# Second layer of an mLSTM / sparse-attention trunk: low parts, scale products, compression products and a mask spread on other places

## The chip, the cores and the metric

One core of one Trainium2 chip. The time is device microseconds of one execution; it is the median of the runs that is compared. The profile is of one execution, and its times are microseconds from the start of the span, unless marked ns.

## The reference

Two layers over 256 tokens of 1024 channels, all float32; then a last norm. Each layer adds a mixer of the normed input:

```python
for i in range(DEPTH):            # DEPTH = 2
    if i % 2 == 0: x = x + mlstm_mixer(rmsnorm(x, ml_norm), ...)
    else:          x = x + nsa_mixer(rmsnorm(x, nsa_norm), ...)
return rmsnorm(x, final_norm)
```

The mLSTM mixer projects to 2 x 2048 channels, convolves, makes q, k and v of four heads, mixes them with exponential gates and projects back with a weight of 2048 x 1024 (the first output projection). The second mixer projects to queries (16 heads of 64), three pairs of keys and values (4 groups of 64), a gate path z and gate logits. One pair is compressed, blocks of 32 tokens at a step of 16:

```python
def compress(t, pe, w1, w2):
    blocks = t[:, tok_idx] + pe[:, None, :]
    flat = blocks.transpose(0, 1, 3, 2, 4).reshape(B, n_cmp, G, CMP_BLOCK * DK)
    return jax.nn.silu(flat @ w1) @ w2
k_cmp = compress(k_c, cmp_pe[0], cmp_w1[0], cmp_w2[0])
v_cmp = compress(v_c, cmp_pe[1], cmp_w1[1], cmp_w2[1])
```

Attention over the compressed pair, over selected blocks and over a window is gated per head, summed, multiplied by SiLU of z and projected by 1024 x 1024.

## The kernel before, in words

Weights come in 44 units of 1 MB or less, each in two halves, through rings of raw tiles (four halves) and of converted tiles (five). `load_unit` issues the load of a half on SyncE's queue (L282); ScalarE rounds it to fp32r, the high part (L283); the low part, raw minus high, is made in one of two ways. Either VectorE subtracts (L289), or ScalarE writes the negated copy (L286) and GpSimd issues a DMA that adds the raw tile to it (L287). The list `BY_DMA` names the halves of the second way. A product of two float32 matrices is then three fp32r products: high by high, low by high, high by low. `next_unit` has two units loaded ahead of the one in use.

Units 0 to 15 are the input projection of the first layer, 16 to 23 its output projection (`out_project`, products at L745, evacuation with the residual at L769). The second layer takes units in the order of `ORDER`: 24 and 25 are the compressed keys and values (`project_tokens`, L828 to L831), 26 to 31 keys and queries in pairs (`heads8`, through `project_channels`, L429), 32 to 35 values and gates, 36 to 39 z, 40 to 43 the output projection.

The norm's factor of a token isn't applied to h: h is x transposed (L345) times the norm's gain, in a high (L350) and a low part (L351), and the factor multiplies the results. `token_scale` makes it by a power on GpSimd (L334), and `token_rows` makes it a row on all partitions by a product of ones with diagonals (L387, L388); rb, rb8, rbh and rp are copies of it, whole, by 1/8, by 1/2 and by the parity of the token.

In `heads8` the first 16 channels of each head are turned: a copy (L852), four small DMAs into a swap tile (L856, on SyncE's queue), two products (L857, and L858 on GpSimd) and an add (L859). There is one swap tile.

`compressed_keys_values` evacuates units 24 and 25 (L1017), transposes, adds the positions into a tile of flat blocks (L1036), multiplies by the first compression weight (L1039) for the keys and then for the values, into the two halves of the partitions of one bank, and so on to a tile `vbd`, in which each group's values are spread over its four heads by a mask (L1066). A plain product of float32 is run in two passes, so one of them stands as two instructions.

The order of instructions on each engine is made by the framework's planner from the program's order and its own estimate of times; `behind(a, b)` sets a after b on their engine, without a semaphore.

Of the kernel before, what the change touches and what calls it, by code (L numbers as in the profile page):

```python
# [12 lines left out]
OP = mybir.AluOpType  # L13
# [3 lines left out]
P = 128  # L17
# [20 lines left out]
MORE = 4  # L38
CG = 1
GV = ((0, 0, 0),)  # L40
VB = 0
NSW = 1

LAG = (0, 4)
# [2 lines left out]
TR = ((0, 0),)  # L47

YH = ((3, 1),)
RBA = 3  # L50
TV = (('px', 'px'), ('acc0', 'acc1'))
TC = ('px', 'px')
TK = (('acc0', 'px'),) * 3
# [10 lines left out]
EDGES = ((1, 8), (1, 32))  # L64
XTH = 2
NOT_POOL = (0, 1, 2, 11)
BOTH = (15, 16, 17)
BY_DMA = [(i, 1) for i in list(range(24)) + list(range(24, 48, 2)) if i not in NOT_POOL] + [(i, 0) for i in BOTH]


WI1 = range(16)
# [136 lines left out]
def trunk(ctx, tc, a, out, dbg=None):  # L208
# [14 lines left out]
    def T(*x, **k):  # L223
        return tile_of(pool[0], *x, **k)
# [42 lines left out]
    def load_unit(src, row, nk, nn):  # L267

        hk = nk // 2
        halves = []  # L270
        for i in range(2):
            raw = TS([P, hk, nn], tag="wr", bufs=WR)
            hi = TS([P, hk, nn], F32R, tag="wh", bufs=WH)
            lo = TS([P, hk, nn], F32R, tag="wl", bufs=WH)
            parts = 1 if loaded else 2
            for j in range(parts):
                if not loaded:
                    load_x(2 * i + j)
                w = hk // parts
                k = slice(j * w, (j + 1) * w)  # L280
                o = i * hk + j * w
                nc.sync.dma_start(raw[:, k, :].rearrange("p k n -> p (k n)"), src[row * P:(row + 1) * P, o * nn:(o + w) * nn])  # L282
                A.activation(hi[:, k, :], raw[:, k, :], AF.Copy)  # L283
                if (len(loaded), i) in BY_DMA:

                    A.activation(lo[:, k, :], raw[:, k, :], AF.Copy, scale=-1.0)  # L286
                    GP.dma_start(out=lo[:, k, :].rearrange("p k n -> p (k n)"), in_=raw[:, k, :].rearrange("p k n -> p (k n)"), accum_op=OP.add)  # L287
                else:
                    V.tensor_tensor(lo[:, k, :], raw[:, k, :], f32(hi[:, k, :]), op=OP.subtract)  # L289
            halves.append((hi, lo))  # L290
        return halves
# [33 lines left out]
    GP.memset(mhalf, -0.5)  # L325


    def rstd_of(ms, n, name):

        k = ms.shape[1]  # L330
        me = T([P, k], name=name + "me")
        V.tensor_scalar(me, ms, 1.0 / n, 1e-6, op0=OP.mult, op1=OP.add)
        r = T([P, k], name=name)
        GP.tensor_tensor(r, me, mhalf[:, 0:k], op=OP.pow)  # L334
        return r

    ahead(N0)
# [9 lines left out]

    def scaled(kts, at, gain):
        for kt in kts:
            A.activation(hh[:, kt, :], at(kt), AF.Copy, scale=gain[:, kt:kt + 1])  # L350
            V.scalar_tensor_tensor(hl[:, kt, :], at(kt), gain[:, kt:kt + 1], f32(hh[:, kt, :]),  # L351
                                   op0=OP.mult, op1=OP.subtract)

# [25 lines left out]

    last = [None]  # L380

    def token_rows(r, bank, **place):

        dg = T([P, 2, P], name="dg", **place)
        ps = PS((P, S), tag=bank)
        for tb in range(2):
            V.tensor_scalar(dg[:, tb, :], ident, r[:, tb:tb + 1], None, op0=OP.mult)  # L387
            last[0] = PE.matmul(ps[:, tb * P:(tb + 1) * P], onesq, dg[:, tb, :], start=True, stop=True)  # L388
        return ps, dg

    held = {}
    rb1 = T([P, S], name="rb1")
    rb1h = T([P, S], name="rb1h")

# [400 lines left out]
    pool[0] = ctx.enter_context(tc.tile_pool(name="s2", bufs=1))  # L795
    transposed(range(4, 8), x_cols, gain2)
    r2 = token_scale(ss2, "r2")
    ps, dg = token_rows(r2, "acc0", tag="p0", bufs=PB)
    rb = T([P, S], name="rb")
    V.tensor_copy(rb, ps)  # L800
    rb8 = T([P, S], name="rb8")
    if RBA & 1:
        A.activation(rb8, ps, AF.Copy, scale=0.125)
    else:
        V.tensor_scalar(rb8, ps, 0.125, None, op0=OP.mult)
    rbh = T([P, S], name="rbh")
    if RBA & 2:
        A.activation(rbh, ps, AF.Copy, scale=0.5)
    else:
        V.tensor_scalar(rbh, ps, 0.5, None, op0=OP.mult)  # L810
    rp = T([P, 2], name="rp")
    V.tensor_tensor(dg, rb.rearrange("p (s r) -> p r s", r=2), ident[:, None, :].to_broadcast([P, 2, P]), op=OP.mult)
    V.tensor_reduce(rp, dg, axis=AX.X, op=OP.add)

    def project_tokens(units, nn, tokens, evac, tags=("px", "px")):

        ps = [PS(tag=t) for t in tags]
        for i, (src, r_) in enumerate(units):
            halves = next_unit(src, r_, nn)
            for k0, low in ((0, False), (0, True), (2, False), (2, True)):  # L820
                for k in (k0, k0 + 1):
                    kt = 4 * i + k
                    hi, lo = halves[k // 2]
                    for t in range(2):
                        lh, ll = tokens(hh, kt, t), tokens(hl, kt, t)
                        o_ = ps[t][:, 0:nn]
                        if low:
                            PE.matmul(o_, lh, lo[:, k % 2, :], start=False, stop=kt == KT - 1)  # L828
                        else:
                            PE.matmul(o_, lh, hi[:, k % 2, :], start=kt == 0, stop=False)  # L830
                            PE.matmul(o_, ll, hi[:, k % 2, :], start=False, stop=False)  # L831
        for t in range(2):
            evac(t, ps[t][:, 0:nn])

# [5 lines left out]
    nc.scalar.dma_start(trig.rearrange("p a s -> p (a s)"), a["rope"])  # L840
    swaps = [T([P, 2, S], name="swap") for _ in range(NSW)]
    for t in swaps:
        GP.memset(t, 0.0)
    turn = lambda i: trig[:, i, None, :].to_broadcast([P, 2, S])

    def heads8(row, rbt, out, n, tags=("px", "px")):
# [167 lines left out]
    def compressed_keys_values():  # L1014
        cs = T([P, 2, G, 2, 64], tag="khl", bufs=2, name="cs")
        project_tokens([(a["wi2"], 0), (a["wi2"], 1)], 512, parity,
                       lambda t, ps: A.activation(cs[:, :, :, t, :], ps.rearrange("p (v g d) -> p v g d", v=2, g=G), AF.Copy,  # L1017
                                                  scale=rp[:, t:t + 1]), tags=TC)
        w1t = []
        for kv in range(2):  # L1020
            for hf in range(2):
# [2 lines left out]
                w1t.append(t)  # L1024
        pe_ = CB("pe").rearrange("p (v l) -> p v l", v=2)
        hps = PS((P, P), tag="acc1")
        for kv in range(2):
            ps = PS((P, G, P), tag="pt")
            for g in range(G):
                PE.transpose(ps[:, g, :], cs[:, kv, g, :, :].rearrange("p r d -> p (r d)"), ident)  # L1030
            f = T([P, 16, G, 16], tag="cf", name="fl")
            GP.memset(f, 0.0)
            for g in range(G):
                src = ps[:, g, 0:128].rearrange("p (c l) -> p l c", l=8)
                for lh_ in range(2):
                    V.tensor_tensor(f[:, 8 * lh_:8 * lh_ + 8, g, 0:15], src[:, :, lh_:lh_ + 15],  # L1036
                                    pe_[:, kv, 8 * lh_:8 * lh_ + 8, None].to_broadcast([P, 8, 15]), op=OP.add)
            for lp in range(16):
                PE.matmul(hps[64 * kv:64 * kv + 64, :], f[:, lp, :, :].rearrange("p g c -> p (g c)"),  # L1039
                          w1t[2 * kv + lp // 8][:, lp % 8, :], start=lp == 0, stop=lp == 15)  # L1040
        h1 = T([P, P], tag="t1", bufs=3, name="h1")
        V.tensor_copy(h1, hps)
# [6 lines left out]
        ps = PS((P, P), tag="acc1")  # L1049
        PE.transpose(ps, h1, ident)  # L1050
        V.tensor_copy(h1T, ps)
        GP.memset(kcb, 0.0)
        ps = PS((P, G, 16), tag="acc1")
        PE.matmul(ps.rearrange("p g c -> p (g c)"), CB("w2k"), h1T[:, 0:64], start=True, stop=True)
        for r in range(2):
# [7 lines left out]
        vc = [T([P, G, 64], F32R, name="vc") for _ in range(2)]  # L1063
        split(*vc, ps)
        for b_, v_ in zip(vbd, vc):
            (GP, V)[VB].tensor_tensor(b_, f32(v_)[:, :, None, :].to_broadcast([P, G, 4, 64]),  # L1066
                             C("hmask")[:, None, :, None].to_broadcast([P, G, 4, 64]), op=OP.mult)

# [128 lines left out]
```

## Time and profile before

| | |
|---|---|
| median of 3 runs | 373.99 us (372.49 to 377.45) |
| the profiled execution | 371.21 us |
| its span | 369.4 us |
| mean granted clock of TensorE | 0.982 of full speed |

The span goes from the first instruction to the last; the time of the execution has what lies around it. A matmul's end is modelled, so the shown idle time before the next one is a lower bound of the time lost.

### The profile page before, as it was taken

How to read it: one execution, taken by the hardware profiler on the slowest of the kernel's cores; microseconds unless marked ns; L12 is line 12 of the kernel's file. 1: busy time of each engine (PE TensorE's matmuls, PEld its weight loads, DVE VectorE, ACT ScalarE, POOL GpSimd, SP SyncE). 2: the span in 40 equal slices, each digit the busy share in tenths (PEclk: the TensorE clock that was granted, in tenths of full speed). 3: DMA queues.
4: the chain of work that ended last, by engine and by line, in shares of the span. 5: the costliest groups of instructions: out<-in, count | busy, mean ns of one | idle time of the engine just before them, and what ended most of it. 6: DMA issues, size and time to landing. Idle time of an engine off the chain costs nothing.

```text
span 369.4 us, 6638 instructions
## 1 busy us (share of the span) xinstructions
PE 348.2 (94%) x2399; PEld 311.4 (84%) x2399; DVE 247.4 (67%) x539; ACT 241.4 (65%) x441; POOL 108.6 (29%) x151
## 2 busy tenths in 40 slices
PE   5999999999999999997997999999699999999991
PEld 5999999999998899875886799999689986777770
DVE  3969977494786789623217547597977989594414
ACT  6755997786696769455736452644589689995304
POOL 1022131322211335010102003671720455665003
PEclk9799999999999999999999999999989999999998
DMA  7899789774569796999998977626496863030003
GB/s 228 323 338 293 221 242 316 171 213 101 188 165 194 219 220 112 267 264 255 261 254 288 301 266 192 158 78 155 134 284 195 268 199 107 2 59 0 2 0 114
DMA packets 23713, 70.62 MB, mean 191 GB/s; under 512 B 2560, under 2 KB 4992, under 8 KB 23680
## 3 DMA queue, kind: packets, MB, share of 16 engines
q1 hardware_dynamic: 17552, 49.76, 39.2%
q0 software_dynamic: 4752, 16.83, 24.9%
q10 hardware_dynamic: 1376, 3.61, 2.9%
q8 instruction: 19, 0.31, 0.3%
q14 instruction: 14, 0.11, 0.1%
HBM read 51.92 MB, written 1.05 MB: 143 GB/s over the span
## 4 chain that ended last, share of the span: by engine, by line
PE 50%; DMA 24%; ACT 11%; DVE 6%; issue 5%; SPq 1%; ACTq 0%; POOLq 0%; POOL 0%; DVEq 0%
PE ps L429 22%; DMA wl<-wr 10%; DMA wr<-in_wo_dram 6%; PE ps L745 6%; ACT wh L283 4%; DMA wr<-in_wi_dram 3%; DVE wl L289 3%; PE ps L664 2%; ACT wl L286 2%; PE ps L1039 2%; PE ps L964 2%; PE ps L952 2%; DMA wr<-in_wi2k_dram 2%; PE ps L548 2%; DMA xch<-in_xt_dram 1%
## 5 line engine op out<-in xcount | busy, mean ns | idle before, releaser
L429 PE MATMUL ps<-hT,wh 128*128 128x256 f32 x832 | 137.5, 291 | 3.4 <-ACT wh L283 3.4
L283 ACT ACTIVATE wh<-wr 128x1024 fp32r<-128x1024 f32 (+2 forms) x90 | 89.9, 1001 | 76.9 <-PE ps L429 28.0
L429 PEld LDWEIGHTS ps<-hT,wh 128*128 128x128 f32 x832 | 120.5, 196 | 5.7 <-ACT wh L283 4.3
L289 DVE TENSOR_TENSOR wl<-wr,wh 128x1024 fp32r<-128x1024 f32 (+2 forms) x57 | 67.7, 1191 | 44.2 <-ACT wh L283 40.9
L429 PE MATMUL ps<-hT,wl 128*128 128x256 f32 x416 | 88.3, 288 | 0.0
L429 PEld LDWEIGHTS ps<-hT,wl 128*128 128x128 f32 x416 | 66.8, 193 | 0.9 <-issue 0.6
L287 POOL DMA_DIRECT2D wl<-wr x33 | 28.7, 879 | 131.5 <-ACT wl L286 120.5
L745 PE MATMUL ps<-wh,r 128*128 128x512 f32 x128 | 35.5, 398 | 1.0 <-DVE x L769 1.0
L286 ACT ACTIVATE wl<-wr 128x1024 fp32r<-128x1024 f32 (+1 forms) x33 | 33.8, 1023 | 2.0 <-DMA wr<-in_wo_dram 2.0
L745 PEld LDWEIGHTS ps<-wh,r 128*128 128x128 f32 x128 | 23.7, 188 | 6.8 <-issue 1.4
L521 DVE SCALAR_TENSOR_TENSOR xc<-xin,pka,xc 128x256 f32<-128x256 f32 x48 | 24.0, 554 | 2.2 <-ACT xc L518 2.2
L745 PE MATMUL ps<-wl,r 128*128 128x512 f32 x64 | 20.1, 398 | 1.4 <-DMA wl<-wr 1.4
L745 PE MATMUL ps<-wh,y 128*128 128x512 f32 x64 | 19.6, 405 | 0.0
L858 POOL TENSOR_TENSOR swap<-swap,trig 128x512 f32<-128x512 f32 x6 | 10.9, 1814 | 20.6 <-DVE qu L852 6.4
L745 PEld LDWEIGHTS ps<-wl,r 128*128 128x128 f32 x64 | 11.9, 188 | 5.1 <-ACT wh L283 1.6
L831 PE MATMUL ps<-wh,hT 128*128 128x280 f32 (+1 forms) x48 | 14.8, 329 | 0.6 <-DVE hT L351 0.6
L901 PE MATMUL ps<-ka,qt 128*128 128x256 f32 (+1 forms) x32 | 12.2, 384 | 2.9 <-DVE nm L907 2.8
L830 PE MATMUL ps<-wh,hT 128*128 128x280 f32 (+1 forms) x48 | 14.9, 330 | 0.0
L745 PEld LDWEIGHTS ps<-wh,y 128*128 128x128 f32 x64 | 11.5, 189 | 2.5 <-issue 0.4
L690 POOL TENSOR_TENSOR xc<-xc,pka 128x1024 f32<-128x1024 f32 x4 | 9.0, 2238 | 13.5 <-PE ps L429 7.6
L745 PE MATMUL ps<-wl,y 128*128 128x512 f32 x32 | 11.1, 401 | 0.0
L902 PE MATMUL ps<-kb,qt 128*128 128x256 f32 (+1 forms) x32 | 11.0, 349 | 0.0
(471 smaller groups left out, 642.6 us busy)
## 6 DMA issues: line engine op xcount, KB each, us to landing
wr<-in_wi_dram SPq DMA_DIRECT2D x34, 512.0 KB
wl<-wr POOLq DMA_DIRECT2D x31, 512.0 KB, 6.0
wr<-in_wo_dram SPq DMA_DIRECT2D x24, 512.0 KB
wr<-in_wi2k_dram SPq DMA_DIRECT2D x12, 512.0 KB
wr<-in_wi2z_dram SPq DMA_DIRECT2D x8, 512.0 KB
wr<-in_wi2v_dram SPq DMA_DIRECT2D x8, 280.0 KB
cw<-in_cw_dram ACTq DMA_DIRECT2D x4, 512.0 KB
xch<-in_xt_dram SPq DMA_DIRECT2D x4, 256.0 KB
```

Of the source, the lines that this page charges most:

```text
L283: A.activation(hi[:, k, :], raw[:, k, :], AF.Copy)
L286: A.activation(lo[:, k, :], raw[:, k, :], AF.Copy, scale=-1.0)
L287: GP.dma_start(out=lo[:, k, :].rearrange("p k n -> p (k n)"), in_=raw[:, k, :].rearrange("p k n -> p (k n)"), accum_op=OP.add)
L289: V.tensor_tensor(lo[:, k, :], raw[:, k, :], f32(hi[:, k, :]), op=OP.subtract)
L429: m = PE.matmul(ps[:, c, :], w, (hl if i == 1 else hh)[:, k, :], start=(k, c, i) == (0, 0, 0), stop=(k, i) == (KT - 1, 2), skip_group_chec ...
L521: V.scalar_tensor_tensor(xc[:, c, :], xin[:, c, tap:tap + S], tap_w(tap, c), xc[:, c, :], op0=OP.mult, op1=OP.add)
L745: PE.matmul(acc, l, r[:, k % 2, cols], start=first and i == 0, stop=last and i == 2)
L830: PE.matmul(o_, lh, hi[:, k % 2, :], start=kt == 0, stop=False)
L831: PE.matmul(o_, ll, hi[:, k % 2, :], start=False, stop=False)
L858: (GP, V)[RE[1]].tensor_tensor(sw, sw, turn(1), op=OP.mult)
L901: PE.matmul(o_, lq, ka[:, g, :, 0:w_], start=True, stop=False)
L902: PE.matmul(o_, lq, kb[:, g, :, 0:w_], start=False, stop=True)
```

## The change

Seven of the halves of units 17 to 23 leave `BY_DMA`, so their low parts are made by VectorE. Conversions of units from 26 on are set behind the last scaling of h on ScalarE. The row-sum products of the second norm and the copies made of them move into the projection of the second compressed unit, behind the high-part products of its first two k tiles (`ROWS_AT`). Four memsets on GpSimd are set behind the power. The two tiles of flat blocks exist at the same time, the second in a slot of the query tiles, and the first compression products alternate between keys and values. The spread of values over heads is made by eight GpSimd operations with a column of the mask as scalar instead of two with the mask as a broadcast operand.

```diff
-BOTH = (15, 16, 17)
-BY_DMA = [(i, 1) for i in list(range(24)) + list(range(24, 48, 2)) if i not in NOT_POOL] + [(i, 0) for i in BOTH]
+ROWS_AT = (1, 0, False)
+BOTH = (15, 16)
+BY_DMA = [(i, 1) for i in list(range(18)) + list(range(24, 48, 2)) if i not in NOT_POOL] + [(i, 0) for i in BOTH]
...
-                A.activation(hi[:, k, :], raw[:, k, :], AF.Copy)
+                conv = A.activation(hi[:, k, :], raw[:, k, :], AF.Copy)
+                if len(loaded) >= 26:
+                    behind(conv, held["hh"])
...
-        GP.tensor_tensor(r, me, mhalf[:, 0:k], op=OP.pow)
+        held["pow"] = GP.tensor_tensor(r, me, mhalf[:, 0:k], op=OP.pow)
...
-            A.activation(hh[:, kt, :], at(kt), AF.Copy, scale=gain[:, kt:kt + 1])
+            held["hh"] = A.activation(hh[:, kt, :], at(kt), AF.Copy, scale=gain[:, kt:kt + 1])
...
-    def token_rows(r, bank, **place):
+    def token_rows(r, bank, product=None, **place):
...
             last[0] = PE.matmul(ps[:, tb * P:(tb + 1) * P], onesq, dg[:, tb, :], start=True, stop=True)
+            if product is not None:
+                behind(last[0], product)
...
-    ps, dg = token_rows(r2, "acc0", tag="p0", bufs=PB)
-    rb = T([P, S], name="rb")
-    V.tensor_copy(rb, ps)
...
+    pow2 = held["pow"]
+    def rows2(product):
+
+        ps, dg = token_rows(r2, "acc0", product, tag="p0", bufs=PB)
+        V.tensor_copy(rb, ps)
         A.activation(rb8, ps, AF.Copy, scale=0.125)
         A.activation(rbh, ps, AF.Copy, scale=0.5)
+        V.tensor_tensor(dg, rb.rearrange("p (s r) -> p r s", r=2), ident[:, None, :].to_broadcast([P, 2, P]), op=OP.mult)
+        V.tensor_reduce(rp, dg, axis=AX.X, op=OP.add)
...
-    def project_tokens(units, nn, tokens, evac, tags=("px", "px")):
+    def project_tokens(units, nn, tokens, evac, tags=("px", "px"), inside={}):
...
+                if (i, k0, low) in inside:
+                    inside[i, k0, low](m)
...
-        GP.memset(t, 0.0)
+        behind(GP.memset(t, 0.0), pow2)
...
-            f = T([P, 16, G, 16], tag="cf", name="fl")
-            GP.memset(f, 0.0)
+            f = T([P, 16, G, 16], tag=("cf", "qt")[kv], bufs=(1, 4)[kv], name="fl")
+            fs.append(f)
+            behind(GP.memset(f, 0.0), pow2)
...
-            for lp in range(16):
-                PE.matmul(hps[64 * kv:64 * kv + 64, :], f[:, lp, :, :].rearrange("p g c -> p (g c)"),
+        for lp in range(16):
+            for kv in range(2):
+                PE.matmul(hps[64 * kv:64 * kv + 64, :], fs[kv][:, lp, :, :].rearrange("p g c -> p (g c)"),
                           w1t[2 * kv + lp // 8][:, lp % 8, :], start=lp == 0, stop=lp == 15)
...
-        GP.memset(kcb, 0.0)
+        behind(GP.memset(kcb, 0.0), pow2)
...
-            (GP, V)[VB].tensor_tensor(b_, f32(v_)[:, :, None, :].to_broadcast([P, G, 4, 64]),
-                             C("hmask")[:, None, :, None].to_broadcast([P, G, 4, 64]), op=OP.mult)
+            for r in range(4):
+                GP.tensor_scalar(b_[:, :, r, :], f32(v_), C("hmask")[:, r:r + 1], None, op0=OP.mult)
```

## Rows read from the trace of the kernel before

**Rows 1.** The page: busy time, share of the span and instructions of each engine.
```profile
PE 348.2 (94%) x2399; PEld 311.4 (84%) x2399; DVE 247.4 (67%) x539; ACT 241.4 (65%) x441; POOL 108.6 (29%) x151
```

**Rows 2.** Busy time by stretches: PE, PEld, DVE, ACT, POOL, clock, DMA share, GB/s.
```profile
140.00:160.00 20.00, 20.00 (x112) 17.22 (x111) 14.83 (x18) 13.78 (x16) 5.58 (x6) 1.00 0.90 223
160.00:180.00 20.00, 17.56 (x79) 13.40 (x78) 4.88 (x5) 11.12 (x14) 2.33 (x4) 1.00 0.92 244
...
260.00:280.00 20.00, 16.54 (x111) 15.28 (x110) 16.73 (x45) 13.94 (x34) 8.86 (x6) 0.91 0.69 198
...
300.00:320.00 20.00, 19.42 (x149) 14.43 (x148) 17.58 (x70) 19.22 (x68) 10.41 (x21) 1.00 0.37 106
```

**Rows 3.** Timeline of TensorE: start, length, instruction, and idle before it.
```profile
165.37 0.47 PE L745 MATMUL ps<-wl,r 128*128 128x512 f32 x1 [0.19 <-DMA wl<-wr]
165.68 0.63 PE L745 MATMUL ps<-wh,r 128*128 128x512 f32 x2
...
169.67 1.17 PE L745 MATMUL ps<-wh,r 128*128 128x512 f32 x4 [1.03 <-DVE x L769]
...
173.45 0.70 PE L745 MATMUL ps<-wl,r 128*128 128x512 f32 x2 [1.21 <-DMA wl<-wr]
...
203.29 0.68 PE L388 MATMUL ps<-dg,onesq 128*128 128x128 f32 x4 [2.20 <-issue]
...
205.06 0.75 PE L831 MATMUL ps<-wh,hT 128*128 128x512 f32 x2 [0.56 <-DVE hT L351]
...
267.11 0.40 PE L901 MATMUL ps<-ka,qt 128*128 128x256 f32 x1 [2.78 <-DVE nm L907]
```

**Rows 4.** The chain that ended last, in order of time: start, length, what.
```profile
318.48 2.34 PE ps L745 x10
```

**Rows 5.** DMA queues: packets, MB, share of 16 engines.
```profile
q1 hardware_dynamic: 17552, 49.76, 39.2%
q0 software_dynamic: 4752, 16.83, 24.9%
```

**Rows 6.** The page's groups, one of them: busy in total, mean ns of one, idle before.
```profile
L289 DVE TENSOR_TENSOR wl<-wr,wh 128x1024 fp32r<-128x1024 f32 (+2 forms) x57 | 67.7, 1191 | 44.2 <-ACT wh L283 40.9
```

**Rows 7.** Timeline of VectorE, first output projection.
```profile
167.70 1.23 DVE L289 TENSOR_TENSOR wl<-wr,wh 128x1024 fp32r<-128x1024 f32 x1 [4.06 <-ACT wh L283]
168.84 1.28 DVE L769 TENSOR_TENSOR x<-ps,x 128x512 f32<-128x512 f32 x2
```

**Rows 8.** Timeline of GpSimd at the second norm.
```profile
200.84 0.96 POOL L1032 MEMSET fl<- 128x1024 f32 x1
...
202.06 0.71 POOL L334 TENSOR_TENSOR r<-r2me,mhalf 128x2 f32<-128x2 f32 x1
```

**Rows 9.** Timeline of VectorE: two operations on two columns.
```profile
137.22 0.17 DVE L681 TENSOR_SCALAR t<-t 128x2 f32<-128x2 f32 x1
...
200.50 1.48 DVE L332 TENSOR_SCALAR r2me<-r2ms 128x2 f32<-128x2 f32 x1
```

**Rows 10.** The chain that ended last, at the second norm.
```profile
202.30 1.06 ACT wh L283
```

**Rows 11.** The chain that ended last: float32 products in two passes.
```profile
63.05 0.45 PE ps L548 x2
...
222.21 3.64 PE ps L1039 x32
...
314.87 1.01 PE ps L964 x8
```

**Rows 12.** Timeline of GpSimd: the spread, and operations with scalars.
```profile
261.76 4.19 POOL L1066 TENSOR_TENSOR vbd<-vc,cst 128x1024 fp32r<-128x1024 f32 x2
...
312.76 1.10 POOL L920 TENSOR_SCALAR p__567_3245<-p__567_3245,sums,gt 128x256 f32<-128x256 f32 x2
```

**Rows 13.** Timeline of VectorE beside the spread.
```profile
261.83 2.37 DVE L859 TENSOR_TENSOR rot<-rot,swap 128x512 f32<-128x512 f32 x1 [0.58 <-POOL swap L858]
```

**Rows 14.** Timeline of VectorE: the next rotation add.
```profile
271.40 0.69 DVE L859 TENSOR_TENSOR rot<-rot,swap 128x512 f32<-128x512 f32 x1 [0.70 <-POOL swap L858]
```

More of the change, by code (lines that the diff above doesn't have):

```diff
@@ L40 @@
 GV = ((0, 0, 0),)
-VB = 0
 NSW = 1
@@ L49 @@
 YH = ((3, 1),)
-RBA = 3
+ROWS_AT = (1, 0, False)
 TV = (('px', 'px'), ('acc0', 'acc1'))
@@ L325, in trunk @@
     GP.memset(mhalf, -0.5)
+    held = {}
     def rstd_of(ms, n, name):
@@ L388, in token_rows @@
             last[0] = PE.matmul(ps[:, tb * P:(tb + 1) * P], onesq, dg[:, tb, :], start=True, stop=True)
+            if product is not None:
+                behind(last[0], product)
         return ps, dg
-    held = {}
     rb1 = T([P, S], name="rb1")
@@ L797, in trunk @@
     r2 = token_scale(ss2, "r2")
-    ps, dg = token_rows(r2, "acc0", tag="p0", bufs=PB)
-    rb = T([P, S], name="rb")
-    V.tensor_copy(rb, ps)
-    rb8 = T([P, S], name="rb8")
-    if RBA & 1:
+    pow2 = held["pow"]
+    rb, rb8, rbh = (T([P, S], name=n) for n in ("rb", "rb8", "rbh"))
+    rp = T([P, 2], name="rp")
+    def rows2(product):
+        ps, dg = token_rows(r2, "acc0", product, tag="p0", bufs=PB)
+        V.tensor_copy(rb, ps)
         A.activation(rb8, ps, AF.Copy, scale=0.125)
[L804 to L807, printed above, removed]
         A.activation(rbh, ps, AF.Copy, scale=0.5)
[L809 to L813, printed above, removed]
-    def project_tokens(units, nn, tokens, evac, tags=("px", "px")):
+        V.tensor_tensor(dg, rb.rearrange("p (s r) -> p r s", r=2), ident[:, None, :].to_broadcast([P, 2, P]), op=OP.mult)
+        V.tensor_reduce(rp, dg, axis=AX.X, op=OP.add)
+    def project_tokens(units, nn, tokens, evac, tags=("px", "px"), inside={}):
         ps = [PS(tag=t) for t in tags]
@@ L830, in project_tokens @@
                             PE.matmul(o_, lh, hi[:, k % 2, :], start=kt == 0, stop=False)
-                            PE.matmul(o_, ll, hi[:, k % 2, :], start=False, stop=False)
+                            m = PE.matmul(o_, ll, hi[:, k % 2, :], start=False, stop=False)
+                if (i, k0, low) in inside:
+                    inside[i, k0, low](m)
         for t in range(2):
@@ L1017, in compressed_keys_values @@
                        lambda t, ps: A.activation(cs[:, :, :, t, :], ps.rearrange("p (v g d) -> p v g d", v=2, g=G), AF.Copy,
-                                                  scale=rp[:, t:t + 1]), tags=TC)
+                                                  scale=rp[:, t:t + 1]), tags=TC, inside={ROWS_AT: rows2})
         w1t = []
@@ L1026, in compressed_keys_values @@
         hps = PS((P, P), tag="acc1")
+        fs = []
         for kv in range(2):
```

## The prediction

> **What bounds the kernel now.** I began with the busy shares: TensorE is busy 94% of the span, the other compute engines 67% and less [rows 1]. So time can come only from the 6% in which TensorE stands, or from products that run at less than the array's pace. The table by stretches says where it stands [rows 2]: in 140 to 180 us the 16 DMA engines are busy 90 to 92%, and of these 40 us the second half has a hole in TensorE (17.56 of 20 us); the next large hole is in 260 to 280 (16.54). VectorE is nearly idle (4.88 of 20) where the DMA engines are full.
>
> The timeline of TensorE gives the holes between 160 and 270 us and who ended each [rows 3]: a low part that came by DMA (0.19 and 1.21), the evacuation of an accumulator (1.03), the row sums of the second norm (2.20, put down to "issue", no wait that the profile can name), the low part of h (0.56), and a score that waited for VectorE (2.78). A matmul is drawn past the moment at which the next can start: ten 512-column products of L745 take 2.34 us, 0.234 each [rows 4], while two are drawn 0.63 long, 0.16 over their pace [rows 3]. So each hole is some 0.17 us longer than shown.
>
> **The change part by part.**
>
> *A. Low parts of the first output projection on VectorE.* Seven half units (the first half of unit 17, the second halves of 18 to 23) lose a ScalarE copy, an issue on POOL's queue and an accumulating DMA, and get one VectorE subtraction. The accumulate queue takes 24.9% of 16 engines for 33 transfers: 0.249 x 369.4 / 33 = 2.8 us of all DMA engines for one (two are smaller). A plain load of 512 KB costs 0.392 x 369.4 us x 0.524 / 49.76 = 1.5 us [rows 5]. A unit here needs two loads and one accumulate, 5.8 us of DMA, against 24 products x 0.234 = 5.6 us of TensorE: hence the DMA share above 0.9. Afterwards it needs 3.0 us, and the stage takes 7 x 2.8 = 20 us less of the DMA engines. VectorE gets 7 x 1.19 = 8.3 us [rows 6], ScalarE loses seven copies as long as a conversion, 7 x 1.06 = 7.4 us [rows 10]; from 140 to 180 alone VectorE has 5 and 15 us free [rows 2], so this lies beside other work. In time, the two waits for low parts (0.19 + 1.21, with 0.17 each 1.7 us) go. The wait for the evacuation, 1.03 + 0.17 = 1.2 us, has the same origin: VectorE stood 4.06 us before a subtraction whose conversion was late, and both evacuations were queued behind it [rows 7]. With early loads the first one runs under the products of the second token block. The second (1.28 / 2 = 0.64 us) can only start when its block ends, and TensorE has two products (0.47 us) for the other bank, so with the signals between engines about 0.4 us stay. A = 1.7 + 0.8 = **2.5 us**; ends 0 (loads late for another reason) and 2.9.
>
> *B. The second norm.* Three edits meet here. The memsets on POOL now stand behind the power: one of them (0.96 us) started at 200.84 and the power only at 202.06 [rows 8], and the two-column VectorE operation before the power took 1.48 us, against 0.17 for one of that kind and size elsewhere [rows 9]. The conversions of unit 26 and later stand behind the scaling of h on ScalarE: the chain of waits now goes through such a conversion, 1.06 us at 202.30 [rows 10], ahead of the columns of h for which TensorE waits. And the row-sum products (some 0.5 us) move into the second compressed unit, behind its first eight products (8 x 0.234 = 1.9 us). Before, TensorE stopped for 2.20 us until the row sums, ran them and one pair of products, and stopped for 0.56. Afterwards it goes on with unit 25 as soon as the first column of h is scaled; a column of 256 needs some 0.4 us on ScalarE and then on VectorE (an estimate: 512 columns take 0.69 there, [rows 14]) and feeds 0.93 us of products. What is queued behind the moved conversions: units 26 and 27, which TensorE needs only after the 24 products of unit 25 and the sums, 6 us, against 1.06 + 1.19 for a half unit. Who waits for the sums: rb, rb8, rbh and rp, first used when the compressed unit or the first key unit is evacuated, 16 products (3.7 us) later. Without that cover the 2.2 us would come back. Holes now: 2.20 + 0.56 + 2 x 0.17 = 3.1 us; 0.3 stay for the first column. B = **2.8 us**.
>
> The row of 1.48 us shows a VectorE operation held while POOL ran memsets. The Trainium skill (SBUF — State Buffer, section "SBUF: two separate sides") calls the port pair that VectorE shares with GpSimd an exclusive lock, held for a whole instruction. By that rule the memsets, which now come right behind the power together with the one for the second tile of flat blocks, hold up what VectorE does then, and B would be about 1.0 us; the trace shows the hold only on the operation ahead of the power.
>
> From rows alone a lower end follows: the hold of 1.3 us (1.48 - 0.17) on the diagonals or the low part of h instead, and half of the added memset's 0.96, take 1.8 from 2.8. So B has the ends **1.0** and 3.1. I stay near the upper one, because the row sums have eight products as cover.
>
> *C. Alternating keys and values.* The 32 first compression products are fp32 in two passes: 64 instructions on half of the array's columns, in two groups of 3.64 us, 0.114 for 128 columns [rows 11]. All keys go first, all values later. Where halves alternate (L964), eight passes of 256 columns take 1.01 us, 0.126 each, against 0.45 / 2 = 0.225 for a pass of 264 columns over the full width [rows 11]: two halves run side by side. At that ratio the 7.28 us become 7.28 x 0.126 / 0.225 = 4.1, at best 3.64: 3.2 to 3.6 saved, or nothing if passes of 128 columns are too short for two weight loads. The products now wait for both transposes and all sixteen additions; products of the key units fill that, as now. C = **3.4 us**, since L964 is the same pattern in the same precision; ends 0 and 3.6.
>
> *D. The spread in eight one-operand pieces.* POOL spends 4.19 us on two three-dimensional products now; two operations of one operand on 128 x 256 take 1.10, so eight pieces 4.4 us [rows 12]: no gain on POOL, and none is needed, as the tile is first read in the output stage. But while the long ones run, VectorE's rotation add takes 2.37 us [rows 13] against 0.69 [rows 14], and a subtraction and the score's minimum come after it; TensorE's hole of 2.78 us begins there. With short pieces VectorE should lose at most one piece: 2.37 - 0.69 - 0.55 = 1.1 us earlier. A loss is possible too: one piece (0.55) more if they hold up one operation more. The swap DMAs of the next unit wait for that add, and behind them on SP's queue stand the loads of z's weights, so what is late next also comes 1.1 earlier. D = **1.1 us**, ends -0.6 and 2.9 (the whole hole).
>
> *At nothing:* RBA goes, with the same code chosen; the second tile of flat blocks takes a slot of the query tiles, whose four are first all asked for by the last query unit, long after the products that read it. The order on every engine is planned anew; what that costs no row shows.
>
> Sum: 2.5 + 2.8 + 3.4 + 1.1 = 9.8 us. Something is given back: later ScalarE works 19.22 and VectorE 17.58 of 20 us (300 to 320) [rows 2], and a TensorE that arrives early meets scores whose softmax is not ready. I take 1 us off. The profiled execution took 371.21 us, 1.8 around its span of 369.4; less 8.8 it is 362.4. The median of the three runs stands 2.8 above it; for a median I forecast 373.99 - 8.8 = **365.2 us**, 2.4% less. Some 2% (7.5 us) is what a measurement of this kernel can tell from no change.
>
> **The rivals.**
> 1. *The gain is lost in the second layer.* The queries go through one swap buffer (copy, four DMAs, POOL product, add), one unit after the other, and the scores through ScalarE. If TensorE comes early and then waits for these, A and half of B remain, 2.5 + 1.4 = 3.9 us: 370. For it: the busy ScalarE. Against it: between 205 and 267 the timeline shows no hole [rows 3], so those chains are not behind now.
> 2. *Pairs don't form, or the memsets hold h.* C = 0 or B = 1.0: 365.2 + 3.4 or + 1.8, 367 to 369.
> 3. *Slower: VectorE's queue blocks in order.* The moved subtractions share a queue with head 3's outputs, the evacuations and the low part of h. Before, one of them stood 4.06 us with the evacuations behind it [rows 7]. If loads stay late, and the point is that one lands after the last product of the unit before, four such places cost 4 us each, 16 us, against the 7.3 that B, C and D bring: 374 + 8.7 = 383. Against it: the accumulates that make loads late are the ones that go.
>
> **How the numbers follow.** Forecast, with 7.5 us or more gained: 0.55. Rival 1: 0.20; rival 2: 0.15 (both within 2%). Rival 3: 0.10, of which 0.07 slower by over 2%. Within 2%: 0.20 + 0.15 + 0.03 = 0.38. The lower end has every term at its upper end, 2.9 + 3.1 + 3.6 + 2.9 = 12.5, and 1.5 for the new order: 360; the upper end takes in rivals 1 and 2: 371.5.
>
> **What would show it.** A: a DMA share below 0.75 in 140 to 180, and no product of L745 that waits for a low part. B: no hole before the row sums, the power ahead of every memset. C: 64 instructions of L1039 in one group of about 3.8 us. D: no VectorE operation held for 1.5 us beside the pieces. The prediction is wrong if holes as large turn up after 210 us, above all before the scores or between z's units.

## The result, and the profile after

The changed kernel takes 370.48 us (median), the kernel before 373.84 in the same session: ratio 0.9924, 95% interval [0.9901, 0.9947]. That is 0.8% less time, where 2.4% was forecast. The profiled execution took 370.49 us; the prediction had 362.4 for it. The time lies inside the range, near its upper end.

The kernels of the runs have line numbers of their own: an instruction of the kernel before stands up to some nine lines further down in the changed one. The page's busy shares and the table by stretches (as in [rows 1, 2]):

```profile
PE 349.8 (95%) x2399; PEld 310.6 (84%) x2399; DVE 255.2 (69%) x546; ACT 236.0 (64%) x434; POOL 110.3 (30%) x150
```

```profile
140.00:160.00 20.00, 20.00 (x113) 17.22 (x112) 19.03 (x23) 12.65 (x15) 3.28 (x3) 1.00 0.76 215
160.00:180.00 20.00, 20.00 (x92) 16.17 (x91) 10.62 (x12) 9.89 (x14) 0.00 (x0) 1.00 0.49 174
...
210.00:220.00 10.00, 8.19 (x64) 7.30 (x64) 4.93 (x17) 3.36 (x4) 0.86 (x1) 0.83 0.70 196
250.00:260.00 10.00, 6.92 (x50) 6.70 (x49) 4.30 (x6) 4.69 (x6) 7.79 (x8) 0.93 0.63 145
260.00:280.00 20.00, 19.54 (x140) 17.89 (x140) 14.69 (x46) 14.84 (x38) 3.43 (x3) 0.95 0.87 259
```

The first layer's half went as forecast: TensorE works all of 140 to 180, and the DMA share fell from 0.90 and 0.92 to 0.76 and 0.49. The prediction's sign of being wrong, holes after 210 us, is there too: in 210 to 220 and 250 to 260 TensorE works 8.19 and 6.92 of 10 us, and the granted clock is 0.83 and 0.93. Before, it worked all of both stretches at full clock. The timeline of TensorE says who ended the waits (as in [rows 3]):

```profile
200.64 0.60 PE L392 MATMUL ps<-dg,onesq 128*128 128x128 f32 x4
...
212.95 1.22 PE L434 MATMUL ps<-hT,wl 128*128 128x256 f32 x8 [1.81 <-DMA wl<-wr]
...
216.03 0.69 PE L1047 MATMUL ps<-cw,fl 128*64 128x128 f32 x2
...
218.76 3.71 PE L1047 MATMUL ps<-cw,fl 128*64 128x128 f32 x62
...
258.26 0.97 PE L829 MATMUL ps<-wl,hT 128*128 128x280 f32 x4 [3.08 <-DMA wl<-wr]
```

The row sums (L392) have no wait any more, against 2.20 us. The 64 instructions of the first compression stand as 2 and 62, and the 62 take 3.71 us where they took twice 3.64 [rows 11]. But two new waits stand in the second layer, both for a low part that comes by DMA: 1.81 us in the first key unit, 3.08 in the first value unit. (The wait of 2.78 us before a score [rows 3] is gone; one of 1.04 us for a softmax operation has come at 286.) GpSimd's timeline shows what issued these DMAs, and when:

```profile
194.68 0.71 POOL L338 TENSOR_TENSOR r<-r2me,mhalf 128x2 f32<-128x2 f32 x1 [9.09 <-DVE r2me L336]
195.34 0.52 POOL L846 MEMSET swap<- 128x512 f32 x1
195.81 1.84 POOL L1038 MEMSET fl<- 128x1024 f32 x2
...
204.91 0.89 POOL L289 DMA_DIRECT2D wl<-wr  x1 [7.12 <-ACT wl L288]
...
245.06 9.79 POOL L1075 TENSOR_SCALAR vbd<-vc,cst 128x256 fp32r<-128x256 f32 x8
254.79 0.86 POOL L289 DMA_DIRECT2D wl<-wr  x1
```

The power now comes first and the memsets behind it. The low part of unit 26, the first key unit, is issued at 204.91, when ScalarE's copy ends; the unit's first product starts 0.3 us later, at 205.21. The low part of the first value unit is issued at 254.79, at the end of the eight pieces of the spread, which take 9.79 us. ScalarE's timeline shows what the copy of unit 26 waited for, four conversions and itself, all behind the scaling of h:

```profile
199.78 3.89 ACT L283 ACTIVATE wh<-wr 128x1024 fp32r<-128x1024 f32 x4
203.56 1.05 ACT L288 ACTIVATE wl<-wr 128x1024 fp32r<-128x1024 f32 x1
```

and the chain that ended last has the DMA itself, and the second one:

```profile
204.91 7.99 DMA wl<-wr
...
254.79 3.42 DMA wl<-wr
```

VectorE's timeline has the operation before the power at 0.17 us (1.48 before, [rows 9]), the diagonals held beside the memsets, and the rotation add beside the pieces at 0.88 (2.37 before, [rows 13]). The diagonals before, then these three after:

```profile
202.80 0.56 DVE L387 TENSOR_SCALAR dg<-pk,r 128x128 f32<-128x128 f32 x2 [0.83 <-POOL r L334]
```

```profile
194.34 0.17 DVE L336 TENSOR_SCALAR r2me<-r2ms 128x2 f32<-128x2 f32 x1
195.42 2.52 DVE L391 TENSOR_SCALAR dg<-pk,r 128x128 f32<-128x128 f32 x2 [0.92 <-POOL r L338]
...
246.19 0.88 DVE L862 TENSOR_TENSOR rot<-rot,swap 128x512 f32<-128x512 f32 x1
```

So each edit does locally what it says, and the end hardly moves. The experiments ask what takes the gain back.

### The profile page after: what moved, and what is told of

It reads as the page before. It is cut to its first block, busy times and chain, and to the rows that moved or that the text cites. A ratio compares the mean times of both kernels' runs of the same rounds, so it can differ in the third digit from the quotient of the medians.

```text
span 368.6 us, 6617 instructions
## 1 busy us (share of the span) xinstructions
PE 349.8 (95%) x2399; PEld 310.6 (84%) x2399; DVE 255.2 (69%) x546; ACT 236.0 (64%) x434; POOL 110.3 (30%) x150
## 3 DMA queue, kind: packets, MB, share of 16 engines
HBM read 51.92 MB, written 1.05 MB: 144 GB/s over the span
## 4 chain that ended last, share of the span: by engine, by line
PE 65%; DMA 10%; DVE 7%; POOL 5%; ACT 5%; issue 5%; SPq 0%; POOLq 0%; DVEq 0%; ACTq 0%
PE ps L434 25%; PE ps L750 18%; DMA wl<-wr 3%; DMA wr<-in_wi_dram 2%; PE ps L967 2%; PE ps L669 2%; POOL vbd L1075 2%; PE ps L955 2%; POOL kb L874 2%; PE ps L904 2%; DMA wr<-in_wi2z_dram 2%; DVE wl L291 2%; DMA wif<-in_wif_dram 2%; PE ps L553 2%; DMA xch<-in_xt_dram 1%
## 5 line engine op out<-in xcount | busy, mean ns | idle before, releaser
L291 DVE TENSOR_TENSOR wl<-wr,wh 128x1024 fp32r<-128x1024 f32 (+2 forms) x64 | 77.7, 1216 | 26.6 <-ACT wh L283 22.2
L289 POOL DMA_DIRECT2D wl<-wr x26 | 22.8, 875 | 116.4 <-ACT wl L288 103.2
L288 ACT ACTIVATE wl<-wr 128x1024 fp32r<-128x1024 f32 (+1 forms) x26 | 26.4, 1015 | 0.0
L861 POOL TENSOR_TENSOR swap<-swap,trig 128x512 f32<-128x512 f32 x6 | 8.8, 1468 | 27.2 <-DMA swap<-kraw 13.8
L831 PE MATMUL ps<-wh,hT 128*128 128x280 f32 (+1 forms) x48 | 15.3, 344 | 0.3 <-ACT hT L354 0.3
L832 PE MATMUL ps<-wh,hT 128*128 128x280 f32 (+1 forms) x48 | 15.2, 341 | 0.0
L829 PE MATMUL ps<-wl,hT 128*128 128x280 f32 (+1 forms) x48 | 11.1, 349 | 3.1 <-DMA wl<-wr 3.1
L938 DVE TENSOR_TENSOR y<-ps,z 128x512 f32<-128x512 f32 (+2 forms) x6 | 3.0, 512 | 14.6 <-PE ps L943 14.6
```

The source lines that it names most:

```text
L832: m = PE.matmul(o_, ll, hi[:, k % 2, :], start=False, stop=False)
```

## Experiments

The kernel before had medians of 373.76 to 374.53 us in these sessions; each ratio is to that of its own session, with its 95% interval. A, B, C and D are the parts of the prediction; a diff already shown ahead of the prediction is only named.

**First set: the two new waits, in the changed kernel.** Theory 1 blamed the pieces on GpSimd, the next one unit 26.

e1_old_spread, part D undone:

```diff
-            for r in range(4):
-                GP.tensor_scalar(b_[:, :, r, :], f32(v_), C("hmask")[:, r:r + 1], None, op0=OP.mult)
+            GP.tensor_tensor(b_, f32(v_)[:, :, None, :].to_broadcast([P, G, 4, 64]), ...)
```

> The changed kernel with the old spread: two broadcast products on GpSimd instead of eight pieces. Theory 1 (the eight pieces hold GpSimd 9.8 us, and the accumulating DMA of a value unit and a swap product queue behind them, which made TensorE's hole of 3.08 us at 258 and the lower clock after it): spread under 5 us, no such hole, 3 to 5 us faster than the changed kernel, 365.5 to 367.5 as a median. Theory 2 (a TensorE that arrives early meets the chain of turned queries anyway): the hole stays in size, within 1.5 us of the changed kernel.

e2_unit26_on_vector, the low part of unit 26 by VectorE, and e3_both, this with e1's edit:

```diff
-NOT_POOL = (0, 1, 2, 11)
+NOT_POOL = (0, 1, 2, 11, 26)
```

> The changed kernel with the low part of the second half of unit 26 on VectorE instead of an accumulating DMA. Theory 1 (setting the conversions behind the scaling of h delayed this DMA to 204.9, it took 8 us, and TensorE waited 1.81 us for it at 212.9 and ran at a lower clock after that): no wait near 211, granted clock 1.00 in 215 to 220, 2 to 3.5 us faster than the changed kernel. Theory 2 (loads are late there for their own sake, the compression weights fill the DMA engines): another wait of 1 to 2 us in 205 to 220, within 1 us of the changed kernel.

> Both edits at once: old spread, and the low part of unit 26's second half on VectorE. Theory 1: the gains add, 5 to 8 us faster than the changed kernel, 363 to 366, ratio to the kernel before 0.970 to 0.980. Theory 2: within 2 us of the changed kernel.

Measured: e1 0.994 [0.9907, 0.9973], e2 0.9992 [0.996, 1.0024], e3 0.9928 [0.9892, 0.9963]. None is faster than the change. In e1 the value unit still waits 2.84 us for its low part, because the old spread, 4.70 us, stands ahead of the issue just as well. In e2 the wait of unit 26 is gone, and others have come: 2.57 and 2.79 us at the small products behind the compression, 3.33 us before a score, 2.12 at a value unit. Theory 1 ("this wait is the loss") fell in all three. Theory 2 gave the time of e1 and e3; e2 is some 2.5 us slower than the change, which neither gave.

**Second set: A, and A with one more part.** s_A_low_parts has only the lists of A:

```diff
-BOTH = (15, 16, 17)
-BY_DMA = [(i, 1) for i in list(range(24)) + ...
+BOTH = (15, 16)
+BY_DMA = [(i, 1) for i in list(range(18)) + ...
```

> The kernel before with part A alone: the seven low parts on VectorE. My sum: no wait of L745 for a low part, DMA share in 140 to 180 below 0.75, the last residual of the first layer 3 to 4 us earlier (193.5 instead of 197), and 2.5 to 4 us faster at the end. Rival (the gain is lost in the second layer): the same start of the second layer, but less than 1.5 us at the end.

a_A_and_B, a_A_and_C and a_A_and_D are that with the diffs of B, C or D; s_B_norm is B without A.

> Part A and part B (the three edits of the second norm) on the kernel before. Theory 3: A alone has no hole of more than 0.5 us at the second norm, so B has nothing left to gain; it brings the compression forward, the spread goes ahead of the first value unit's DMA on GpSimd's queue, and the time is 1 to 5 us longer than A alone. The prediction's step B: 2.8 us faster than A alone.

> Part A and part C (alternating products) on the kernel before. Theory 3 (with the compression finished earlier, the spread is planned on GpSimd's queue ahead of the accumulating DMA of the first value unit; TensorE then waits for that low part): the products of L1039's place take 3.6 us instead of 7.3, but a hole of 2 to 3 us before a low-part product of the value units near 250, and no more than 2 us faster than A alone (365.8), or slower. Theory 2 (the gain of C is simply lost to the turned queries): about A alone, with a hole before the first scores instead.

> Part A and part D (eight pieces) on the kernel before. The spread stays behind the first value unit's DMA on GpSimd's queue. Theory 3: eight pieces of 0.9 us or more, 7 to 10 us of GpSimd; only the second value unit's DMA and the last swap product are behind them, so 0 to 3 us slower than A alone. My prediction's step D: 1 us faster than A alone.

> Part B alone on the kernel before. The prediction's step B: 2.8 us faster (0.9925), the hole of 2.2 us before the row sums gone. Theory 4: that hole goes, but the accumulating DMA of unit 26 comes late as in the changed kernel and TensorE waits for it, so 0 to 6 us slower, 1.000 to 1.015.

Measured: A alone 365.8 us, **0.9775** [0.9725, 0.9825]; with B 0.9989 [0.9952, 1.0026]; with C 0.9811 [0.9749, 0.9874]; with D 0.9803 [0.9731, 0.9875]; B alone 1.0105 [1.0066, 1.0143]. A alone brings more than the whole change and more than was expected of it, and B takes it all back, more than theory 3's 1 to 5 us. The prediction's gain from B didn't come; D's 1 us is too small to be told by these intervals. In A with C the spread does stand ahead of the value unit's DMA, as theory 3 has it, but TensorE waits only 0.78 us for that low part, and 2.30 for an evacuation. TensorE and GpSimd in A alone, at the second norm:

```profile
198.01 0.68 PE L388 MATMUL ps<-dg,onesq 128*128 128x128 f32 x4 [0.16 <-PE ps L345]
...
200.66 2.38 PE L429 MATMUL ps<-hT,wh 128*128 128x256 f32 x18
```

```profile
196.78 0.71 POOL L334 TENSOR_TENSOR r<-r2me,mhalf 128x2 f32<-128x2 f32 x1
197.44 0.88 POOL L287 DMA_DIRECT2D wl<-wr  x1
```

The wait of 2.20 us before the row sums is down to 0.16 with no edit at the norm, and they start 5.28 us earlier. The low part of unit 26 is issued at 197.44, 3.2 us ahead of the unit's first product at 200.66, against 0.3 us in the changed kernel. And that product stands inside unit 25: the rest of unit 25 follows it.

**Third set: where the spread stands, and the order of conversions.** f1_late_old_spread has the old spread called later and set behind the accumulating DMA of unit 34 on GpSimd; b3_change_no_conv_order is the change, and b1_A_B_no_conv_order A and B, without `behind(conv, held["hh"])`; b2_A_conv_order is A with that line alone.

```diff
+            behind(GP.tensor_tensor(b_, f32(v_)[:, :, None, :].to_broadcast([P, G, 4, 64]), ...), adds[34])
```

> The whole change, but the spread in its old form of two products, and set on GpSimd behind the accumulating DMA of the second value unit. Theory 3: no hole above 1 us before a low part of the value units, 3 to 6 us faster than the changed kernel, 364 to 367. Theory 2: the time of the changed kernel within 1.5 us, the hole only moves.

> The whole change, without the order that sets the conversions of units from 26 on behind the scaling of h. Theory 4 (part B is what costs, and in it this order: it holds four conversions and the accumulating DMA of unit 26 until h is scaled, so the first key unit ends 3.5 us later and with it the serial chain of the turned keys and queries): no wait of 2 us for a low part near 211, the first key unit evacuated by 212 instead of 214.2, 3 to 6 us faster than the changed kernel. Rival theory 5 (the place of the row-sum products is what costs: the compressed unit is finished before unit 26 begins): within 1.5 us of the changed kernel, the first key unit still after 213.

> Parts A and B without the order of the conversions: the row sums inside the second compressed unit and the memsets behind the power stay. Theory 4: near A alone (0.9775), 0.975 to 0.982 of the kernel before. Theory 5: near A and B (0.9989), above 0.992.

> Part A and of part B the order of the conversions alone. Theory 4: a wait of about 2 us for the low part of unit 26 near 211, and a ratio near A and B, 0.990 to 1.000. Theory 5: near A alone, 0.975 to 0.982.

Measured: f1 0.9943 [0.9909, 0.9977], no gain over the change or e1 (theory 3 fell; the wait at the value unit shrank to 1.41 us, and one of 5.03 came before a score); b3 0.9952 [0.9921, 0.9983]; b1 0.9937 [0.9913, 0.9961]; b2 **1.0126** [1.0081, 1.0171]. The one line costs A 3.5%, more than theory 4 gave. But in b1 and b3 theory 5 holds: with the row sums inside unit 25 the line costs nothing that can be told from zero. There TensorE begins unit 26 behind unit 25 (206.71 and 206.47 us), not inside it as in A alone, with the line or without. And in b3 TensorE waits 6.38 us for the low part of a value unit:

```profile
259.87 1.30 PE L827 MATMUL ps<-wl,hT 128*128 128x280 f32 x4 [6.38 <-DMA wl<-wr]
```

That low part starts to be used at 258.26 us in the changed kernel and at 259.87 in b3: the eight pieces stand ahead of its DMA on GpSimd in both, so what TensorE gains before it ends as a longer wait.

**Fourth set: which edit of B, by which mechanism.** g1_A_memsets is A with the memsets behind the power; g2_A_rows_inside A with the row sums inside unit 25; g3_A_conv_from_27 is b2 with

```diff
-                if len(loaded) >= 26:
+                if len(loaded) >= 27:
```

and g4_A_C_D is the change with B alone undone.

> Part A and, of the second norm's edits, the memsets behind the power alone. Theory 4 (the loss of B on top of A comes from products placed on TensorE's queue ahead of their inputs; the memsets only hold two VectorE operations on the diagonals by some 2 us): nearly A alone, ratio 0.977 to 0.985. Rival (the memsets hold VectorE at the norm, as the port-lock rule has it, and this is the loss): the diagonals for the row sums end some 2.3 us later and TensorE stands for them, ratio 0.985 to 0.995.

> Part A and the row sums inside the second compressed unit alone, with no memset and no conversion moved. Theory 4: this is what costs 6 us of the 1.6% that rows and memsets cost together on A (the evacuations of the compressed units and the second compression products come later than TensorE's queue has them): ratio 0.990 to 0.996, holes of over 1.5 us near 242 and 285 us. Rival (memsets): ratio within 0.4% of A alone, 0.975 to 0.982, no such hole.

> Part A and the order of conversions behind h, but from unit 27 on, so that unit 26, the first key unit, is free of it. A and the order from unit 26 on was 1.0126. Theory 4a (what costs is unit 26: its copy and its accumulating DMA come after h, and the first key unit starts late): the first key unit is evacuated near 211 us again and the ratio is 0.975 to 0.985. Rival (any order that puts conversions behind h on ScalarE moves the whole plan of the second layer, unit 27 too): ratio above 0.99.

> The change with part B alone undone: A, C and D. A and C was 0.9811, A and D 0.9803. Theory (B is the part that loses what A brings, C and D are worth nothing on A): 0.975 to 0.985, so undoing B is worth 1 to 2% of the changed kernel's 0.9924. Rival (C and D together pile operations on the value units as in the changed kernel, with the hole before L829 and the half clock after it, whatever B does): 0.988 to 0.995.

Measured: g1 0.9765 [0.9708, 0.9822], g2 0.9935 [0.9901, 0.9968], g3 0.977 [0.971, 0.983], g4 0.9883 [0.9823, 0.9942].

g1: the memsets cost nothing at the end. g3 against b2: the whole 3.5% of the conversion order goes through unit 26. GpSimd and TensorE in b2, then GpSimd in g3:

```profile
205.54 0.89 POOL L289 DMA_DIRECT2D wl<-wr  x1 [8.83 <-ACT wl L288]
```

```profile
215.96 0.62 PE L431 MATMUL ps<-hT,wl 128*128 128x256 f32 x3 [2.62 <-DMA wl<-wr]
```

```profile
197.50 0.88 POOL L289 DMA_DIRECT2D wl<-wr  x1
```

The DMA for unit 26 is issued 8 us later in b2, TensorE waits 2.62 us for it, and the first key unit is evacuated at 222.7 instead of 210.3 us. Most of that is not the wait: behind it 32 of the compression's instructions (5.37 us) stand on TensorE's queue ahead of the key unit's last products.

g2: the place of the row sums costs A 1.6%. VectorE, GpSimd and TensorE in g2:

```profile
234.92 3.00 DVE L858 TENSOR_TENSOR rot<-qu,trig 128x512 f32<-128x512 f32 x1
...
238.15 3.10 DVE L872 TENSOR_TENSOR kb<-rot,ka 64x1024 fp32r<-64x1024 f32 x1
...
242.73 1.22 DVE L872 TENSOR_TENSOR kb<-rot,ka 64x1024 fp32r<-64x1024 f32 x1
...
244.59 0.45 DVE L1057 COPY kcb<-ps 64x64 f32<-64x64 f32 x2
```

```profile
234.78 5.40 POOL L872 TENSOR_TENSOR kb<-rot,ka 64x1024 fp32r<-64x1024 f32 x2
```

```profile
242.00 0.40 PE L432 MATMUL ps<-hT,wh 128*128 128x256 f32 x2
245.19 1.94 PE L1063 MATMUL ps<-pkb,h1r 128*128 128x64 f32 x8 [2.79 <-DVE kcb L1057]
...
247.24 0.63 PE L432 MATMUL ps<-hT,wh 128*128 128x256 f32 x2
```

The last products of the compression, those of the values (L1063), stand on TensorE's queue ahead of the rest of a query unit. They are written into the bank (acc1) from which a copy of the compressed keys (L1057) still has to read, and VectorE has that copy queued behind rotations and keys. Those take 3.00 and 3.10 us while GpSimd makes its keys, and 1.22 (the same operation) after it. TensorE waits 2.79 us, and the next pair of products takes 0.63 instead of 0.40: the granted clock over 240 to 250 is 0.75. In A alone the same products start at 252.06, after the keys, and in A with C at 233.10, before GpSimd begins them at 233.83, both without a wait:

```profile
252.06 1.00 PE L1062 MATMUL ps<-pkb,h1r 128*128 128x64 f32 x8
```

```profile
233.10 1.00 PE L1067 MATMUL ps<-pkb,h1r 128*128 128x64 f32 x8
```

The same wait of 2.1 to 2.8 us is in A with B (2.18), in b1 (2.16), e2 and e3 (2.79 each). It isn't all that g2 loses: TensorE waits another 2.25 us at 288.51, and the first key unit is evacuated at 213.59 instead of 210.85, since it begins behind unit 25.

g4: theory 4 missed here, and its rival holds. With B undone TensorE waits 6.27 us at the first value unit, and GpSimd shows why:

```profile
258.70 1.30 PE L828 MATMUL ps<-wl,hT 128*128 128x280 f32 x4 [6.27 <-DMA wl<-wr]
```

```profile
242.49 10.11 POOL L1072 TENSOR_SCALAR vbd<-vc,cst 128x256 fp32r<-128x256 f32 x8
252.55 0.86 POOL L287 DMA_DIRECT2D wl<-wr  x1
```

C ends the compression some 10 us earlier (its result is copied at 221.4 us; in A alone at 231.8), so the spread comes ahead of the value unit's accumulating DMA on GpSimd's queue, and D makes it 10.11 us long. In A with D, the pieces start only at 257.2, behind that DMA. TensorE uses this low part from 258.70 us on, as late as in the changed kernel: undoing B alone moves the time into this wait.

**Fifth set.** h1_A_C_D_late_pieces is g4 with the pieces set behind unit 34's DMA, with f1's edit; s_C_alternate is the kernel before with C alone.

> A, C and D with the eight pieces of the spread set behind the accumulating DMA of unit 34 on GpSimd. With A, C and D the pieces stood ahead of the accumulating DMA of the first value unit (pieces from 242.49 for 10.11 us, the DMA issued at 252.55) and TensorE waited 6.27 us for that low part; the ratio was 0.9883. Theory 5 (D costs through GpSimd's queue, but only where C brings the spread ahead of that issue): the hole of 6 us goes, 4 to 6 us come back, ratio 0.973 to 0.980. Rival (the value units are late for their loads and conversions, as A and C shows with 0.9811): the hole shrinks to 2 to 4 us and the ratio stays at 0.981 to 0.988.

> The kernel before with part C alone. My step said 3.4 us (ratio 0.991) from the kernel as it was. Rival (the products take half as long, but what is next on the path was late anyway, so the 3.6 us end as waits between 240 and 300 us): ratio 0.997 to 1.003, one group of some 3.7 us of compression products in the timeline.

Measured: h1 0.9811 [0.9735, 0.9887], 367.8 us. It lies below g4's 0.9883, with intervals that overlap, at the lower end of what the rival gave. In its trace (an execution of 371.68 us, well above the median) the wait of 6.27 us is gone, and one of 2.05 us for a low part from VectorE stands in its place, as the rival has it. So the queue made most of g4's wait; that it made the lost time isn't settled. s_C **1.0149** [1.0101, 1.0196], 380.2 us, beyond both expectations. TensorE's timeline in it:

```profile
226.90 3.71 PE L1044 MATMUL ps<-cw,fl 128*64 128x128 f32 x62
...
238.49 0.30 PE L1055 MATMUL ps<-pk,h 128*128 128x128 f32 x1 [2.29 <-DVE h L1052]
...
248.63 1.94 PE L1067 MATMUL ps<-pkb,h1r 128*128 128x64 f32 x8 [2.79 <-DVE kcb L1061]
```

The products take half as long, and of the small products behind them two groups wait 2.29 and 2.79 us, the second for the same copy as in g2. 3.6 us are won and 5.1 lost there; TensorE works 7.21 of 10 us in 240 to 250, and the granted clock is 0.77 in 250 to 260. Later waits of 1.76 (a value unit's low part) and 2.04 us (before a z unit) are new too. So a compression that ends earlier lands its small products beside the making of the keys here. On A it ends before the keys, without that wait, which fits that C costs 5.6 us alone and nothing clear on A.

## Why the prediction was wrong, step by step

**The step that failed is the sum itself: four terms added, with "The order on every engine is planned anew; what that costs no row shows" entered at nothing.** The 1 us taken off for the second layer was all that stood against it. Measured one by one, the parts change the time by -8.4 us (A), +3.9 (B), +5.6 (C), and on A by about +8.0 (B), +1.3 (C, not told from zero) and +1.0 (D, not told from zero): ratios times 374; D alone was not run. They don't add up to the change's -2.8. That they don't is shown by the runs; that each moves instructions into the way of another is read from the traces.

*A was too small.* Forecast 2.5; alone it brings 8.4 us by the ratio, 6.5 to 10.3 by its interval, and 5.6 between the two profiled executions, 371.21 and 365.58 (before's median lies 2.8 above its profile, as the prediction said). Its three waits in the first layer went as forecast. What was missed: the power of the second norm comes at 196.78 instead of 202.06 [rows 8], since the last residual is earlier, and with it goes the hole of 2.20 us that the prediction put down to B. The sum counted 2.5 + 2.8 = 5.3 for the two; A alone brings that and more. The rest isn't explained. The trace of before may show less than a usual execution loses: in s_C, whose edit lies behind the first layer, the waits for low parts are 1.05 and 1.69 us and the one before the row sums 2.71.

*B was taken for +2.8 and is a loss.* Its local claims came true: the power ahead of the memsets, no hole before the row sums. The step "units 26 and 27, which TensorE needs only after the 24 products of unit 25 and the sums, 6 us, against 1.06 + 1.19 for a half unit" failed twice. The second half of unit 26 is in `BY_DMA`: behind its conversion come a copy of 1.05 us, an issue, and a DMA of 7.99 us, not a subtraction of 1.19. And A's plan starts unit 26 inside unit 25. g3 against b2 shows that this costs 3.5% on A. The place of the row sums costs 1.6% on A (g2); that it does so through the products at L1063 is read from the trace and was not isolated, for no run moved them alone. The two don't add: B as a whole costs A 2.1%, and with the row sums inside unit 25 the order of conversions costs nothing clear (b1 against A with B, b3 against the change).

The two VectorE operations on the diagonals took 2.52 us beside the memsets, against 0.56 in the kernel before. The Trainium skill (SBUF — State Buffer, section "SBUF: two separate sides") has VectorE and GpSimd share a port pair under an exclusive lock for a whole instruction, by which the prediction named 1.0 as B's value. The trace agrees with the hold. In g1, with one memset less, they took 1.63 us, and it cost nothing: they end at 198.39, and the row sums, at 198.53, stand behind transposes, not behind them.

*C was right in size at its place* (7.28 us to 3.7) *and wrong in what it brings.* The prediction asked what the products wait for, not who comes after them. Behind them come the small products on TensorE's queue, and behind those the spread on GpSimd's.

*D was mis-sized and its queue forgotten.* 0.55 us for a piece was read off a group of the same size that writes plain float32 [rows 12]; the eight pieces, which write fp32r rows with gaps, took 9.79 us, 1.2 each, against 4.4. "No gain on POOL, and none is needed" left out the DMAs that GpSimd issues behind the pieces, though for B the prediction did ask what is queued behind the moved conversions. VectorE's add did come down to 0.88, as forecast.

*The rivals.* Rival 1 gave 370 and named the second layer as the place where the gain is lost; that is the time that came, though hardly its chain: the changed kernel's two large waits are for low parts, and one of 1.04 us is for softmax. So its number is luck. Rival 2's memsets held VectorE and cost nothing, and its pairs did form. Rival 3 didn't happen: VectorE took the seven subtractions without one wait of TensorE in 160 to 176.

*What stays open.* In the changed kernel no single edit undone is clearly faster: e1, b3 and f1 lie at 0.994 to 0.995, the change at 0.9924, and g4 (B undone) at 0.9883 with an interval that overlaps; C alone undone was not run. It is clearly so only with two parts undone (A and C, 0.9811; A and D, 0.9803), with B undone and the pieces late (h1, 0.9811), or with all but A undone (0.9775). How the 4.9 us between the profiled executions of A alone and of the change divide was not settled. The two waits and the clock after them are some 8.6 us (1.81 + 3.08, and 0.17 x 10 + 0.07 x 10 + 0.05 x 20 = 3.4 for the clock, with 0.17 for each wait). C gives 3.6 back, and A alone has two waits of its own that the change lacks:

```profile
262.17 0.36 PE L901 MATMUL ps<-ka,qt 128*128 128x256 f32 x1 [2.79 <-DVE nm L907]
...
268.32 0.51 PE L429 MATMUL ps<-hT,wh 128*128 128x256 f32 x2 [1.73 <-ACT wh L283]
```

That leaves 8.6 - 3.6 - 4.5 = 0.5 us, so most of the 4.9 isn't accounted for by these.

A alone, g1 and g3 are the fastest that were run (0.9775, 0.9765, 0.977) and aren't told apart.

## What to carry to other kernels

When one edit brings work forward, first ask which later waits vanish by that alone, and don't price them again under another edit. A step that makes a chain end earlier is worth its time only if the next operations of that chain find their engines free; follow it to the next product on an in-order queue and to everything that its engine issues, DMAs above all. Where a planner orders the engines from the program, an order forced by hand at one place should be tested alone, and on top of each other edit.

## What the runs showed of the hardware

- Eight one-operand GpSimd operations on 128 x 256 with a strided output took 8.73 to 10.14 us in six runs (9.79 in the changed kernel, 10.11 in g4), about twice the 3.79 to 4.70 of two broadcast products on 128 x 1024 that do the same (4.19 in the kernel before, [rows 12]).
- A VectorE operation of 1.22 us took 3.10 in g2 while GpSimd ran products of the same kind.
- Around some waits of TensorE the granted clock over 10 us was lower: 0.83 with 1.81 us in the changed kernel, 0.75 with 2.79 in g2, where two products took 0.63 us for 0.40 (2.4 GHz is 1.00; the other level, 1.2 GHz, 0.50). Around others it stayed 1.00, as around the 2.20 us before the row sums in the kernel before and the 2.79 in A alone.
